# Softmax without the division: the reciprocals of the sums travel as rows through DRAM and scale the gates

## The chip, the cores and the metric

One core of a Trainium2 chip runs the kernel. The metric is the device time of the whole program in microseconds, the median of several runs. The engines are TensorE (PE; its weight loads are listed as PEld), VectorE (DVE), ScalarE (ACT), GpSimd (POOL) and SyncE (SP), which here issues all DMAs.

## The reference, cut to what matters

A layer over 1024 tokens of width 1024. Two token mixers run beside each other, each with 8 heads of 64 output columns; their outputs are gated by silu, projected, gated by a sigmoid and added.

```python
# mixer A: a chunk of 64 queries sees its own and 8 earlier chunks
s = jnp.einsum('bqhd,bkhd->bhqk', qc, kc).astype(jnp.float32) * scale + bias
p = jax.nn.softmax(s, axis=-1).astype(vc.dtype)
ya = jnp.einsum('bhqk,bkhd->bqhd', p, vc)
ya = (ya.reshape(B, S, A_WIDTH) * jax.nn.silu(a_z)) @ w_proj_a[l]
# mixer B: chunk-causal, all earlier chunks, low-rank q and kv
yb = chunk_causal_attention(q_full, k_full, kv[..., B_NOPE_DIM:])
yb = (yb.reshape(B, S, B_WIDTH) * jax.nn.silu(b_z)) @ w_proj_b[l]
mixed = jax.nn.sigmoid(g_a) * ya + jax.nn.sigmoid(g_b) * yb
```

The softmax divides each row of exponentials by its sum. The division may be done anywhere between the exponential and the projection, since it is one factor per token and head; the gate silu(z) is such a factor, too.

## The kernel before, in words

The first 110 us normalise the input and make V of mixer A and the low-rank parts of B. Then come two attention stretches, A and B, in which "dense" matmuls (the chunks of the input projection: q, k, z of each pair of heads and the output gates) are woven between the attention steps as filler for TensorE. Then the two output projections, the product with w_out and the last normalisation follow.

Heads go in pairs (four pairs per mixer; e is the head in the pair). A head has 8 steps, i = 0 to 7, each for 128 query tokens. Steps 0 to 3 are the first token half (512 tokens), steps 4 to 7 the second. In a step, `scores` makes the scores in PSUM, VectorE adds the bias (A) or masks (B) and finds the row extreme (L717, L816), and `softmax` (L825) does the rest: ScalarE takes Exp and the row sum (L828), VectorE makes 2^14 over the sum (L830, L831), ScalarE writes the high f16 half of P (L835, "hi"), VectorE the low half (L836, "lo"), and a DMA transpose issued by SyncE brings both into pT (L838). `pv` (L841) multiplies V with pT. It runs LAG_A = 3 steps (A) or LAG_B = 2 steps (B) behind the scores, from the queue of class Steps (L858). After the fourth PV of a half, `finish_y` takes y out of PSUM (L741, L742) and `finish_z` multiplies it with the gate sz on GpSimd (L748) and stores it to DRAM (L750), from where the projection's operand is loaded later. Only the last two heads of B stay on the chip (L752).

The gate sz of a pair is 128 rows (64 per head) by 512 tokens for each half. It comes from a dense chunk (`evac_silu`, L728), and its pool has two buffers. Scratch tiles of 512 columns (zt, yl, yt, weights and gates) share the ring `st` of five buffers. GpSimd also scales the bias table of each A head (L700 to L702) and splits V of B into f16 halves (L548, L551) in two stretches.

The order of the emitted steps is written out by hand (`run`, `at`, and the constants ahead of the function); the order on each engine is then settled by the framework's scheduler, which simulates the program's times.

Of the kernel before, what the change touches and what calls it, by code (L numbers as in the profile page):

```python
# [10 lines left out]
F32 = mybir.dt.float32  # L11
F32R = mybir.dt.float32r
I32 = mybir.dt.int32
AF = mybir.ActivationFunctionType
ALU = mybir.AluOpType
# [3 lines left out]
P = 128  # L19
S = 1024  # L20
# [35 lines left out]
def tile_hybrid_layer(  # L56
# [25 lines left out]
    V, A, G, SY = nc.vector, nc.scalar, nc.gpsimd, nc.sync  # L82
# [10 lines left out]
    st = ctx.enter_context(tc.tile_pool(name="st", bufs=5))  # L93
    sm = ctx.enter_context(tc.tile_pool(name="sm", bufs=6))
# [3 lines left out]
    dram = ctx.enter_context(tc.tile_pool(name="dram", bufs=1, space=DRAM))  # L98
# [3 lines left out]
    kr_d = [dram.tile([32, S], F32, name=f"kr_d{i}") for i in range(2)]  # L102
    y_d = [dram.tile([512, S], F32, name=f"y_d{i}") for i in range(2)]
    th_d = [dram.tile([D, S], F32, name=f"th_d{i}") for i in range(2)]


    ident = consts.tile([P, P], F32, name="ident")
# [102 lines left out]
    def start_ya():  # L210

        if not YA:
            tiles = {}

            def one(k, half):
                if (k // 2, 0) not in tiles:
                    for a in range(2):
                        tiles[k // 2, a] = m8.tile([P, 2, S], F32R, tag="m8", name=f"YA{k // 2}{a}")
                for a in range(2):
                    YT[0][a] = YT[0][a] or {}  # L220
                    YT[0][a][k] = tiles[k // 2, a][:, k % 2, :]
                y_part(0, k, half, YT[0][0][k], YT[0][1][k])

            YA.extend([(0, lambda k=k, half=half: one(k, half)) for k in range(4) for half in range(2)])
        return YA
# [33 lines left out]
    def proj_a(ds_):  # L259

        def one(d, half):
            ahead(0, d, half, st, AH0)
            if half == 0:
                if d < 7:
                    prep_p(0, d + 1)
                else:
                    prep_p(1, 0)
                if d % 4 == 0:
                    t = big.tile([P, 4, S], F32, tag="big", name=f"ya{d // 4}")
                    for a in range(4):  # L270
                        ya[d + a] = t[:, a, :]
            proj(0, d, half, ya[d][:, half * 512 : half * 512 + 512])

        return [(2.6, lambda d=d, half=half: one(d, half)) for d in ds_ for half in range(2)]
# [34 lines left out]
    if True:  # L309
# [203 lines left out]
        def v_units(g, v16, mixer, nm, lo_eng, ring, mx=None):  # L513
# [39 lines left out]
            def done():  # L553
                V16[2 * mixer + g] = v16

            return [(0, pre)] + [(0, lambda j=j: one(j)) for j in range(NT)] + [(0, done)]

        ln_last = {}
# [88 lines left out]
    with ExitStack() as p1:  # L647
# [88 lines left out]
        def finish_y(pair, mixer, e, half):  # L736
            h = 2 * pair.p + e
            lo = st.tile([P, 512], F32, tag="st", name=f"yl{mixer}_{h}_{half}")
            yt = st.tile([P, 512], F32, tag="st", name=f"yt{mixer}_{h}_{half}")
            r = slice(64 * e, 64 * e + 64)  # L740
            A.activation(lo[0:64, :], pair.y[64:128, :], AF.Copy, scale=us[mixer][64:128, h : h + 1])  # L741
            V.scalar_tensor_tensor(yt[r, :], pair.y[0:64, :], us[mixer][0:64, h : h + 1], lo[0:64, :], op0=ALU.mult, op1=ALU.add)  # L742
            pair.tail(e, half, yt, r)
# [78 lines left out]
            def tail(self, e, half, yt, r):  # L822
                finish_z(self, 1, e, half, yt, r)

        def softmax(pair, e, i, nm_):  # L825
            s, nm, n = pair.scores(e, i)
            su = sm.tile([P, 1], F32, tag="su", name=f"su{nm_}")
            A.activation(s[:, :n], s[:, :n], AF.Exp, scale=-1.0, bias=nm, accum_out=su)  # L828
            rc2 = sm.tile([P, 1], F32, tag="rc2", name=f"rcs{nm_}")
            V.tensor_scalar(rc2, su, 2.0 ** -14, None, op0=ALU.mult)  # L830
            V.reciprocal(rc2, rc2)  # L831
            W_ = pools["w"]
            p16 = pools["p"].tile([P, 2 * W_], F16, tag="p16", name=f"p16{nm_}")
            hi, lo = p16[:, :n], p16[:, n : 2 * n]
            A.activation(hi, s[:, :n], AF.Copy, scale=rc2)  # L835
            V.scalar_tensor_tensor(lo, s[:, :n], rc2, hi, op0=ALU.mult, op1=ALU.subtract)  # L836
            pT = pools["pt"].tile([P, 2 * W_ // P, P], F16, tag="pt", name=f"pT{nm_}")
            SY.dma_start(pT[:, : 2 * n // P, :], p16[:, : 2 * n], transpose=True)  # L838
            return pT

        def pv(pair, mixer, e, i, pT, v16):  # L841
            h = 2 * pair.p + e
            k0 = max(0, i - 4) if mixer == 0 else 0
            if i % 4 == 0:
                pair.y = ps_y.tile([P, 512], F32, tag="y", name=f"y{mixer}_{h}_{i}")
            nk = i - k0 + 1
            o = pair.y[:, (i % 4) * P : (i % 4) * P + P]
            for k in range(nk):
                for a in range(2):
                    T.matmul(o, v16[:, k0 + k, h % 4, :], pT[:, a * nk + k, :], start=(k == 0 and a == 0), stop=(k == nk - 1 and a == 1))  # L850
            if i % 4 == 3:
                finish_y(pair, mixer, e, i // 4)
# [5 lines left out]
        class Steps:  # L858
# [7 lines left out]
            def one(self):  # L866
                pair, e, i = self.seq[self.at]
                self.at += 1
                nm = f"{self.m}_{2 * pair.p + e}_{i}"
                self.q.append((pair, e, i, softmax(pair, e, i, nm)))  # L870
                if i == 6:
                    self.next_head()
                if len(self.q) > self.lag:
                    self.fin()
# [5 lines left out]

            def fin(self):
                pair, e, i, pT = self.q.pop(0)
                pv(pair, self.m, e, i, pT, V16[2 * self.m + pair.p // 2])

            def units(self, n):
# [100 lines left out]
        with ExitStack() as pb:  # L986
# [7 lines left out]
            for p in range(4):  # L994
                u = sb.units(16)
                if p < 3:
                    n = pairsB[p + 1]
# [110 lines left out]
    for j in range(NT):  # L1108
        n = 4 if j == last else 2
# [68 lines left out]
```

## Time and profile before

| | us |
|---|---|
| median of 3 runs | 876.08 (873.44 to 879.13) |
| the profiled execution | 874.21 |
| its span, first to last instruction | 872.4 |
| TensorE busy | 821.9 |
| VectorE busy | 592.2 |
| ScalarE busy | 443.0 |
| GpSimd busy | 197.6 |

All rows come from the one profiled execution. "Busy" is the time in which an engine has an instruction running; for TensorE it includes pipelined overlap. "Idle <- X" is the time that an engine stood still just before an instruction, put down to the X that ended it last.

### The profile page before, as it was taken

The page shows a single profiled execution, that of the slowest core. Times are in us where ns is not written, and L with a number is a line of the kernel's source. Part 1 is how long each engine was busy: PE and PEld are TensorE (multiplying, and loading weights), DVE is VectorE, ACT ScalarE, POOL GpSimd, SP SyncE. Part 2 cuts the span into 40 slices and gives each one's busy share as a digit, 9 for nine tenths or more (in the row PEclk, how much of TensorE's full clock was granted, in tenths as well). Part 3 has the DMA queues.
Part 4 walks back from the last instruction along what each step waited for, and adds up shares of the span by engine and source line. Part 5 has one row for each costly group of instructions (what it writes and reads, how often), then busy time and mean ns, then how long its engine had stood idle before and what let it go on. Part 6 is the DMA issues. An engine that isn't in the chain of part 4 may idle for free. (4 is left out here: it accounts for less than half of the span.)

```text
span 872.4 us, 13717 instructions
## 1 busy us (share of the span) xinstructions
PE 821.9 (94%) x4760; PEld 691.5 (79%) x4760; DVE 592.2 (68%) x1351; ACT 443.0 (51%) x857; POOL 197.6 (23%) x205
## 2 busy tenths in 40 slices
PE   5999999998998998999999999999999989999996
PEld 4999898887776876787778778787888778888886
DVE  6899856587686889845565767276637674647755
ACT  4223683476675857755563666366647552322000
POOL 6545630011111113400000521010213131331100
PEclk8999999999999999999999999999999999999999
DMA  6622023476877775674639377746886798541421
GB/s 210 209 106 77 13 62 109 142 149 141 165 138 168 139 178 96 135 202 102 152 96 200 80 166 159 162 102 140 192 199 173 186 217 289 161 151 49 160 94 48
DMA packets 185365, 124.68 MB, mean 143 GB/s; under 512 B 146161, under 2 KB 149745, under 8 KB 185297
## 3 DMA queue, kind: packets, MB, share of 16 engines
q1 hardware_dynamic: 185296, 123.82, 57.0%
q8 instruction: 37, 0.61, 0.3%
q14 instruction: 32, 0.25, 0.1%
HBM read 57.98 MB, written 22.81 MB: 93 GB/s over the span
## 5 line engine op out<-in xcount | busy, mean ns | idle before, releaser
L173 PE MATMUL dn<-hT,wh_c 128*128 128x512 f32 x512 | 204.8, 400 | 2.0 <-ACT g L294 1.3
L175 PE MATMUL dn<-hT,wl_c 128*128 128x512 f32 x512 | 201.5, 394 | 0.0
L174 PE MATMUL dn<-hT,wh_c 128*128 128x512 f32 x512 | 201.4, 393 | 0.0
L748 POOL TENSOR_TENSOR yt<-yt,sz 64x512 f32<-64x512 f32 x32 | 43.6, 1362 | 328.0 <-DVE yt L742 263.8
L173 PEld LDWEIGHTS dn<-hT,wh_c 128*128 128x128 f32 x512 | 97.0, 190 | 20.2 <-ACT g L294 1.8
L175 PEld LDWEIGHTS dn<-hT,wl_c 128*128 128x128 f32 x512 | 96.7, 189 | 20.0
L174 PEld LDWEIGHTS dn<-hT,wh_c 128*128 128x128 f32 x512 | 97.0, 189 | 17.6
L132 DVE TENSOR_TENSOR wl_c<-wr_c,wh_c 128x512 fp32r<-128x512 f32 x64 | 47.8, 746 | 77.4 <-ACT wh_c L131 71.2
L131 ACT ACTIVATE wh_c<-wr_c 128x512 fp32r<-128x512 f32 x64 | 40.2, 629 | 82.4 <-DMA wr_c<-in_wch_dram 63.2
L836 DVE SCALAR_TENSOR_TENSOR p<-sbs,rcs,p 128x128 f16<-128x128 f32 (+3 forms) x64 | 57.1, 901 | 24.2 <-ACT p L835 22.3
L828 ACT ACTIVATE sbs<-sbs,nmb 128x128 f32<-128x128 f32 (+3 forms) x64 | 49.5, 774 | 33.4 <-DVE sbs L816 30.1
L836 DVE SCALAR_TENSOR_TENSOR p<-ss,rcs,p 128x640 f16<-128x640 f32 (+2 forms) x64 | 50.7, 803 | 9.2 <-ACT p L835 8.1
L828 ACT ACTIVATE ss<-ss,nm 128x640 f32<-128x640 f32 (+2 forms) x64 | 44.3, 692 | 23.1 <-DVE nm L717 20.6
L835 ACT ACTIVATE p<-sbs,rcs 128x128 f16<-128x128 f32 (+3 forms) x64 | 48.5, 769 | 12.8 <-ACT sbs L828 6.8
L850 PE MATMUL y<-pT,v16b 128*128 128x128 f16 x576 | 43.7, 222 | 9.8 <-DMA pT<-p 9.8
L175 PE MATMUL ops<-wo,mixT 128*128 128x512 f32 (+1 forms) x144 | 52.9, 367 | 0.0
L850 PEld LDWEIGHTS <-v16b 128*128 128x128 f16 x576 | 33.9, 99 | 23.8 <-issue 22.2
L174 PE MATMUL ops<-wo,mixT 128*128 128x512 f32 (+1 forms) x144 | 52.7, 366 | 0.0
L173 PE MATMUL ops<-wo,mixT 128*128 128x512 f32 (+1 forms) x144 | 51.5, 368 | 0.0
L816 DVE TENSOR_SCALAR_CACHE_REDUCE sbs<-sb 128x128 f32<-128x128 f32 (+3 forms) x64 | 47.9, 754 | 1.3
L717 DVE CUSTOM_DVE_ANT_0 ss<-sa,tb 128x640 f32<-128x640 f32 (+2 forms) x64 | 41.3, 652 | 8.9 <-PE sa L713 5.2
L850 PE MATMUL y<-pT,v16a 128*128 128x128 f16 x480 | 37.4, 220 | 9.6 <-DMA pT<-p 9.6
(248 smaller groups left out, 1847.8 us busy)
## 6 DMA issues: line engine op xcount, KB each, us to landing
wr_c<-in_wch_dram SPq DMA_DIRECT2D x64, 256.0 KB, 3.2
th_d<-g SPq DMA_DIRECT2D x32, 256.0 KB, 2.9
th<-th_d SPq DMA_DIRECT2D x32, 256.0 KB, 3.7
h_d<-xt SPq DMA_DIRECT2D x8, 512.0 KB, 2.6
sX<-sQ SPq DMA_DIRECT2D x16, 256.0 KB, 4.2
sXb<-bQ SPq DMA_DIRECT2D x16, 256.0 KB, 4.3
r<-h_d SPq DMA_DIRECT2D x8, 512.0 KB, 3.6
wor<-in_wo_dram SPq DMA_DIRECT2D x16, 256.0 KB, 3.0
```

Of the source, the lines that this page charges most:

```text
L131: A.activation(hi, raw, AF.Copy)
L132: (eng or V).tensor_tensor(lo, raw, f(hi), op=ALU.subtract)
L173: T.matmul(ps, ah, bh, start=start, stop=False)
L174: T.matmul(ps, ah, bl, start=False, stop=False)
L175: return T.matmul(ps, al, bh, start=False, stop=stop).ins
L717: V.tensor_tensor_reduce(s[:, :n].rearrange("p (b w) -> p b w", b=nb), ps[:, :nb, :w], self.tb[e][:, 640 - n : 640].rearrange("p (b w) -> ...
L748: G.tensor_tensor(yt[r, :], yt[r, :], pair.sz[half][r, :], op=ALU.mult)
L816: V.tensor_scalar(s[:, :n].rearrange("p (b w) -> p b w", b=nb), ps[:, :nb, :w], -B_SCALE, None, op0=ALU.mult, op1=ALU.min, accum_out=nm,)
L828: A.activation(s[:, :n], s[:, :n], AF.Exp, scale=-1.0, bias=nm, accum_out=su)
L835: A.activation(hi, s[:, :n], AF.Copy, scale=rc2)
L836: V.scalar_tensor_tensor(lo, s[:, :n], rc2, hi, op0=ALU.mult, op1=ALU.subtract)
L850: T.matmul(o, v16[:, k0 + k, h % 4, :], pT[:, a * nk + k, :], start=(k == 0 and a == 0), stop=(k == nk - 1 and a == 1))
```

## The change

P is no longer divided by its row sums. hi and lo are the exponentials times the constant 2^14. The sums of four steps gather in the four columns of one tile. After the fourth step VectorE takes their reciprocals in one instruction, and GpSimd issues a DMA that writes them as a row of 512 tokens to a DRAM tile (`sums_out`). Two steps later (at i = 5 for the first half, at i = 1 of the next head for the second) `norm` issues, again from GpSimd, a read of that row broadcast to 64 partitions, and GpSimd multiplies the gate sz by it in place. `finish_z` is as before, so y is divided there by way of the gate. The last half of a mixer is normed in `fin`, just ahead of its PV product.

```diff
+    rc_d = [dram.tile([8, S], F32, name=f"rc_d{i}") for i in range(2)]
...
-        def softmax(pair, e, i, nm_):
+        def softmax(mixer, pair, e, i, nm_):
             s, nm, n = pair.scores(e, i)
-            su = sm.tile([P, 1], F32, tag="su", name=f"su{nm_}")
-            A.activation(s[:, :n], s[:, :n], AF.Exp, scale=-1.0, bias=nm, accum_out=su)
-            rc2 = sm.tile([P, 1], F32, tag="rc2", name=f"rcs{nm_}")
-            V.tensor_scalar(rc2, su, 2.0 ** -14, None, op0=ALU.mult)
-            V.reciprocal(rc2, rc2)
+            if i % 4 == 0:
+                sums[pair, e] = sm.tile([P, 4], F32, tag="su", name=f"su{nm_}")
+            su = sums[pair, e]
+            A.activation(s[:, :n], s[:, :n], AF.Exp, scale=-1.0, bias=nm, accum_out=su[:, i % 4 : i % 4 + 1])
...
-            A.activation(hi, s[:, :n], AF.Copy, scale=rc2)
-            V.scalar_tensor_tensor(lo, s[:, :n], rc2, hi, op0=ALU.mult, op1=ALU.subtract)
+            A.activation(hi, s[:, :n], AF.Copy, scale=2.0 ** 14)
+            V.scalar_tensor_tensor(lo, s[:, :n], 2.0 ** 14, hi, op0=ALU.mult, op1=ALU.subtract)
...
+            if i % 4 == 3:
+                sums_out(mixer, pair, e, i // 4, su)
...
+        def sums_row(mixer, pair, e, half):
+            return rc_d[mixer][2 * pair.p + e : 2 * pair.p + e + 1, half * 512 : half * 512 + 512]
...
+        def sums_out(mixer, pair, e, half, su):
...
+            rc = sm.tile([P, 4], F32, tag="rc", name=f"rc{nm}")
+            V.reciprocal(rc, su)
+            G.dma_start(sums_row(mixer, pair, e, half).rearrange("o (a b) -> (o b) a", a=4), rc)
+            open_.add((pair, e, half))
...
+        def norm(mixer, pair, e, half):
...
+            r = slice(64 * e, 64 * e + 64)
+            rb = st.tile([P, 512], F32, tag="st", name=f"rb{nm}")
+            G.dma_start(rb[r, :], sums_row(mixer, pair, e, half).broadcast_to([64, 512]))
+            G.tensor_tensor(pair.sz[half][r, :], pair.sz[half][r, :], rb[r, :], op=ALU.mult)
...
-                self.q.append((pair, e, i, softmax(pair, e, i, nm)))
+                self.q.append((pair, e, i, softmax(self.m, pair, e, i, nm)))
+                if i in (1, 5) and self.at > 2:
+                    past = self.seq[self.at - 3]
+                    norm(self.m, past[0], past[1], past[2] // 4)
...
             def fin(self):
                 pair, e, i, pT = self.q.pop(0)
+                if i % 4 == 3 and (pair, e, i // 4) in open_:
+                    norm(self.m, pair, e, i // 4)
```

## Rows read from the trace of the kernel before

**Rows 1.** The page's head and its first part: span, and busy time by engine.
```profile
span 872.4 us, 13717 instructions
PE 821.9 (94%) x4760; PEld 691.5 (79%) x4760; DVE 592.2 (68%) x1351; ACT 443.0 (51%) x857; POOL 197.6 (23%) x205
```
**Rows 2.** Table of stretches: length, busy time by engine, granted clock, DMA share, GB/s.
```profile
168.00:396.00 228.00, 213.91 (x1338) 175.90 (x1337) 172.32 (x418) 154.70 (x304) 43.50 (x55) 0.99 0.70 148
396.00:722.00 326.00, 309.92 (x1800) 254.29 (x1800) 201.53 (x503) 187.40 (x342) 53.89 (x46) 0.99 0.68 156
```
**Rows 3.** TensorE's waits: total us, how many, the longest.
```profile
PE y L850 <- DMA pT<-p: 19.4, 23, 2.4
...
PE sa L712 <- DVE nm L717: 3.7, 2, 2.3
PE sb L809 <- DVE sbs L816: 3.5, 4, 2.0
...
PE sb L809 <- DVE rcs L830: 1.3, 1, 1.3
```
**Rows 4.** Timeline of one softmax step of mixer A: start, length, engine, instruction.
```profile
238.09 0.19 ACT L828 ACTIVATION_READ_ACCUMULATOR ss<-ss,nm 128x1 f32 x1
...
238.31 0.15 DVE L830 TENSOR_SCALAR rcs<-su 128x1 f32<-128x1 f32 x1
...
238.50 0.16 DVE L831 RECIPROCAL rcs<-rcs 128x1 f32<-128x1 f32 x1
...
238.74 0.83 ACT L835 ACTIVATE p<-ss,rcs 128x640 f16<-128x640 f32 x1 [0.47 <-ACT ss L828]
```
**Rows 5.** Groups by line and shape: busy us, mean ns of one, idle before.
```profile
L831 DVE RECIPROCAL rcs<-rcs 128x1 f32<-128x1 f32 x128 | 20.7, 163 | 3.4
...
L830 DVE TENSOR_SCALAR rcs<-su 128x1 f32<-128x1 f32 x128 | 19.2, 151 | 26.6 <-ACT sbs L828 17.7 <-ACT ss L828 7.0
...
L550 ACT ACTIVATE v16b<-vs_b 128x256 f16<-128x256 f32 x16 | 6.2, 405 | 0.1
...
L835 ACT ACTIVATE p<-sbs,rcs 128x256 f16<-128x256 f32 x8 | 4.0, 501 | 2.7 <-issue 1.6 <-ACT sbs L828 1.1
```
**Rows 6.** Timeline of TensorE: first and last of the 23 waits for pT.
```profile
177.39 0.38 PE L850 MATMUL y<-pT,v16a 128*128 128x128 f16 x4 [0.79 <-DMA pT<-p]
...
713.46 0.72 PE L850 MATMUL y<-pT,v16b 128*128 128x128 f16 x10 [1.90 <-DMA pT<-p]
```
**Rows 7.** Groups by line: two of GpSimd's products.
```profile
L748 POOL TENSOR_TENSOR yt<-yt,sz 64x512 f32<-64x512 f32 x32 | 43.6, 1362 | 328.0 <-DVE yt L742 263.8 <-DVE rcs L830 18.5 <-DVE sb L813 17.9
...
L548 POOL TENSOR_TENSOR vs_b<-v16b,vsc_b 128x256 f32<-128x256 f32 x16 | 15.2, 958 | 31.5 <-ACT vsc_b L539 28.5 <-DVE sz L733 2.4 <-DVE wl_kn L132 0.2
```
**Rows 8.** Timeline at the end of a mixer A half: an issue on SyncE, the sum.
```profile
240.43 0.42 SPq L699 DMA_DIRECT2D tb<-in_relb_dram  x1
...
241.05 0.19 ACT L828 ACTIVATION_READ_ACCUMULATOR ss<-ss,nm 128x1 f32 x1
```
**Rows 9.** DMA: packets, queue with its share of 16 engines, issues with landing times.
```profile
DMA packets 185365, 124.68 MB, mean 143 GB/s; under 512 B 146161, under 2 KB 149745, under 8 KB 185297
...
q1 hardware_dynamic: 185296, 123.82, 57.0%
...
y_d<-yt SPq DMA_DIRECT2D x28, 128.0 KB, 2.5
...
pT<-p SPq DMA_TRANSPOSE x128, 3.4
```
**Rows 10.** The view of the tile pT, its landing line.
```profile
DMA to landing us min/median/max: 2.3/3.4/6.8
```
**Rows 11.** Timeline: the gate product of that half, and B's last sum and gate product.
```profile
253.90 1.81 POOL L748 TENSOR_TENSOR yt<-yt,sz 64x512 f32<-64x512 f32 x1 [8.39 <-DVE yt L742]
...
711.96 0.19 ACT L828 ACTIVATION_READ_ACCUMULATOR sbs<-sbs,nmb 128x1 f32 x1
...
724.91 1.29 POOL L748 TENSOR_TENSOR yt<-yt,sz 64x512 f32<-64x512 f32 x1 [11.93 <-DVE yt L742]
```

More of the change, by code (lines that the diff above doesn't have):

```diff
@@ L834, in softmax @@
             hi, lo = p16[:, :n], p16[:, n : 2 * n]
-            A.activation(hi, s[:, :n], AF.Copy, scale=rc2)
-            V.scalar_tensor_tensor(lo, s[:, :n], rc2, hi, op0=ALU.mult, op1=ALU.subtract)
+            A.activation(hi, s[:, :n], AF.Copy, scale=2.0 ** 14)
+            V.scalar_tensor_tensor(lo, s[:, :n], 2.0 ** 14, hi, op0=ALU.mult, op1=ALU.subtract)
             pT = pools["pt"].tile([P, 2 * W_ // P, P], F16, tag="pt", name=f"pT{nm_}")
             SY.dma_start(pT[:, : 2 * n // P, :], p16[:, : 2 * n], transpose=True)
-            return pT
+            if i % 4 == 3:
+                sums_out(mixer, pair, e, i // 4, su)
+            return pT
+        sums, open_ = {}, set()
+        def sums_row(mixer, pair, e, half):
+            return rc_d[mixer][2 * pair.p + e : 2 * pair.p + e + 1, half * 512 : half * 512 + 512]
+        def sums_out(mixer, pair, e, half, su):
+            nm = f"{mixer}_{2 * pair.p + e}_{half}"
+            rc = sm.tile([P, 4], F32, tag="rc", name=f"rc{nm}")
[3 more added lines that the diff above has]
+        def norm(mixer, pair, e, half):
+            nm = f"{mixer}_{2 * pair.p + e}_{half}"
+            open_.remove((pair, e, half))
+            r = slice(64 * e, 64 * e + 64)
+            rb = st.tile([P, 512], F32, tag="st", name=f"rb{nm}")
+            G.dma_start(rb[r, :], sums_row(mixer, pair, e, half).broadcast_to([64, 512]))
+            G.tensor_tensor(pair.sz[half][r, :], pair.sz[half][r, :], rb[r, :], op=ALU.mult)
         def pv(pair, mixer, e, i, pT, v16):
```

## The prediction

> **What bounds the kernel now.** I read the page's first part, then the table of stretches, then TensorE's waits, then one softmax step in the timeline. TensorE is busy for 821.9 of 872.4 us [rows 1], so at most 50 us can be had from it, and only where it waits. The change works in the two attention stretches alone, from 168 to 396 us (mixer A) and from 396 to 722 us (mixer B). There TensorE is busy for 213.9 of 228 and 309.9 of 326 us [rows 2]: 30.2 us idle. VectorE (172 and 202 us), ScalarE (155 and 187 us) and GpSimd (43 and 54 us) have room on the average. What matters is therefore the latency of a step, not the sum of its work. The table of TensorE's waits says which latency: 19.4 us in 23 waits of the PV product for its transposed P (pT), then 8.5 us in 7 waits of the scores matmul for VectorE (3.7 + 3.5 + 1.3) [rows 3]. So the last link ahead of TensorE is the chain Exp, reciprocal, hi, lo, transpose.
>
> **What the change removes.** In each of the 128 steps, ScalarE's hi copy waits for two tiny VectorE instructions on the sum. The timeline of a step shows it: the accumulator read ends at 238.28, the scaling runs at 238.31, the reciprocal at 238.50, and hi starts only at 238.74, with an idle of 0.47 us put down ahead of it [rows 4]. After the change hi depends on Exp alone, which ran before it on the same engine: 0.46 us of latency is gone. hi's scale also becomes a constant. Two ScalarE copies of 128x256 to f16 differ in just that: 405 ns without a scale from memory, 501 ns with one [rows 5]. I take 0.09 us; zero is the lower end. lo's scalar becomes a constant too, which I take at nothing. A step's pT is then ready 0.55 us earlier. VectorE loses 128 x (151 + 163 ns) = 40.2 us [rows 5] and gets 32 reciprocals of four columns back, 32 x 0.163 = 5.2 us.
>
> **What that is worth on TensorE.** I went through the 23 waits for pT one by one (the first is 0.79 us, the last 1.90 us [rows 6]) and took from each the smaller of its length and 0.55 us: 13 are longer and give 7.2 us, the 10 shorter ones sum to 3.0 us. That is 10.2 us. The waits for VectorE shrink by at most the 0.31 us that each step sheds there: 7 x 0.31 = 2.2 us. Together 12.4 us. The ends are 27.9 us (all these waits gone) and 0: the order of instructions on each engine is laid out by a planner that simulates the kernel, and a planner that sees pT earlier may put the PV product earlier, so that it waits as long as before.
>
> **What it adds on GpSimd.** Per token half and head (32 in all) there are two DMA issues, two waits on landings, and one 64x512 product. The product is the same shape as the gate product that runs now, 1362 ns [rows 7], so 43.6 us in all. A DMA issued by GpSimd does not occur before the change. The nearest row is an issue on the SyncE queue, 0.42 us [rows 8]. [...] I take 0.42 us, since that row is the same kind of instruction: 64 x 0.42 = 27 us. GpSimd then works 97 + 44 + 27 = 168 of 554 us, plus waits. From the sum to the scaled gate the chain is 0.16 (reciprocal) + 0.42 + 2.5 (landing of the store of y to DRAM) + 0.42 + 3.4 (landing of pT, for the broadcast read) + 1.36 = 8.3 us [rows 5, 7 to 9]. The cover is the time from the end of the accumulator read of a half's last step to the gate product that needs the result: 241.24 to 253.90 = 12.7 us in A, and 712.15 to 724.91 = 12.8 us at the very end of B [rows 8, 11]. So 4.4 us are left and I cost the chain at nothing. With both landings at 6.8 us it is 16.0 us and the gate product comes 3 us late. That product feeds a store whose reader comes much later, and at the end of B TensorE has projections to run. What is queued behind a waiting GpSimd is the bias table of the next head and the splitting of V, on which a ScalarE copy waits. By the code that is 16 products of L548 (0.96 us [rows 7]), one per step, in 16 of the 128 steps: 32 x 16/128 = 4 halves fall there. At 5.9 us of landings each, that is at most 24 us on ScalarE. TensorE would see a part of it, because PV runs two or three steps behind the scores. I take 0 and keep 10 us for the range. The broadcast tile also holds one of the five buffers of `st`, for 0.42 + 3.4 + 1.36 = 5.2 us: 32 x 5.2 = 166 of 5 x 554 buffer-us, 6%. At nothing, too; without that cover ScalarE's evacuation of a dense chunk would wait for a buffer and hold one of the two dense PSUM tiles. The gate must be there one step earlier than now. Its dense chunk is the first of a pair, and its first half is four of some 24 units, so it lies well ahead of step 5.
>
> **What it adds on the DMA engines.** They are busy for 0.70 and 0.68 of the two stretches [rows 2], so this is the fullest resource after TensorE. A row of sums goes out as 512 elements of 4 bytes, each a packet of its own, 32 on each of 16 engines. A mean packet now takes 0.57 x 872.4 us x 16 / 185296 = 43 ns [rows 9], so a scatter takes 1.38 us of every engine. The broadcast read of 128 KB runs at 156/0.68 = 229 GB/s [rows 2], 0.57 us. That is 1.95 us per half, 62 us in all, and the share goes to about 0.80. It falls on the resource that delivers pT. TensorE waits for 23 of 128 pT, 18%. If every scatter and read holds one pT up for its whole length, 32 x 1.95 x 0.18 = 11.2 us come back; if the packets slip between, none. I take the middle, 5.6 us. SyncE's own queue gains no instruction, and its pT issues, which wait for lo, come earlier.
>
> **The sum.** 874.2 us (the profiled execution; span 872.4 and 1.8 around it) - 12.4 + 5.6 = 867.4 us. The profiled execution is 1.9 us under the median of 876.08, so against the median the forecast is 869 us, 0.8% faster.
>
> **Rivals.**
> *The gain is replanned away.* TensorE is 94% busy, and a planner may spend a shorter chain on an earlier PV product. For it: the waits now are short (19.4 us in 23) although each step's chain has some microseconds, so the order already sits close to the data. Against it: the waits come from landings later than planned, and the change shortens the part that the landing follows. Time: 876, or up to 880 with some of the packet cost.
> *The whole of it comes through.* Less waiting, VectorE 35 us lighter and no packet cost: 876 - 12.4 = 864; with half of the other waits, (27.9 - 12.4)/2 = 8 us, gone as well, 856.
> *The scatter is dear, and the kernel ends slower.* The mechanism is one: packets of 4 bytes hold the DMA engines while pT is in flight. With the same half weight it decides where 32 x 0.18 x 0.5 x (32 p + 0.57 us) = 12.4 us, at p = 117 ns a packet, 2.7 times today's mean. At 250 ns it is 8.57 us per half and 24.7 us back: 876 + 12 = 888 us. At 150 ns the engines' free 31% (172 us, 5.4 us per half) would be used up as well. For it: no packet of 4 bytes written to DRAM is in this trace. Against it: the mean of 43 ns is made mostly of small ones, 146161 of 185365 being under 512 B [rows 9]. [...]
> [...]
> *That it does not do what it says* would be a hi copy that still waits for VectorE; the diff leaves it no such operand, so I give this no chance of its own.
>
> **How the numbers follow.** Forecast (862 to 873) 0.45; replanned away (873 to 881) 0.20; everything comes through (852 to 862) 0.14; dear packets or a GpSimd that holds ScalarE (881 to 900) 0.21. A change of 1% (8.8 us) is about what a measurement of this kernel can tell from none. Under 867.3 us lie the whole third case and somewhat under half of the first, 0.14 + 0.21 = 0.35. Over 884.8 us lies most of the last, 0.17. Between them is 0.48. The range leaves out the outer parts of the two end cases: 857 to 888.
>
> **What the profile after would show.** Right: the idle ahead of the hi copy for VectorE gone, the two tiny lines replaced by 32 reciprocals, PV's waits for pT near 9 to 15 us, scores waits under 7 us, GpSimd near 240 us busy with the gate's scaling ending before the gate product starts, DMA share near 0.80. Replanned: the same shorter steps, but PV's waits as long as now. Dear packets: a second DMA queue with some 16000 packets and a large share of the engines, and the median landing of pT well over 3.4 us. The prediction is wrong where GpSimd's issue of 512 elements takes many microseconds, so that the chain passes 12.7 us, or where ScalarE shows new waits for GpSimd in the V stretches.

## The result: 1051.5 us, 19.8% slower

The changed kernel takes 1051.53 us (median of 4 runs, 1043.12 to 1057.87) against 877.61 us (4 runs, 873.44 to 880.02): a ratio of 1.1975, 95% interval 1.1916 to 1.2035. The forecast was 869 us with 888 us as its upper end.

The profiled execution after the change has a span of 1041.3 us. The head of its page, and its DMA queues (packets, MB, share of 16 engines), answer to [rows 1, 9]:

```profile
span 1041.3 us, 13686 instructions
...
PE 878.4 (84%) x4760; PEld 733.3 (70%) x4760; DVE 567.5 (54%) x1127; ACT 434.3 (42%) x857; POOL 287.1 (28%) x301
...
DMA packets 187924, 128.94 MB, mean 124 GB/s; under 512 B 147696, under 2 KB 151280, under 8 KB 187856
...
q1 hardware_dynamic: 185296, 123.82, 61.3%
q0 software_dynamic: 2560, 4.26, 2.2%
```

TensorE idles 162.9 us in place of 50.5, and the same 4760 matmuls are busy for 56.5 us longer. The old queue q1 moves the same 185296 packets and the same 123.82 MB as before, but each holds its engine for 0.613 x 1041.3 x 16 / 185296 = 55 ns on the average, 43 ns before [rows 9]. The new queue q0 takes only 2.2%. So the new transfers take little of the engines by themselves, and the old ones take longer; that the first causes the second is shown under spread below.

The stretches of mixers A and B, now 308 and 408 us long (228 and 326 before [rows 2]; the columns are the length, the busy us of TensorE, its weight loads, VectorE, ScalarE and GpSimd, the granted clock, the DMA share and GB/s):

```profile
168.00:476.00 308.00, 241.34 (x1329) 197.47 (x1328) 161.51 (x305) 149.71 (x302) 87.15 (x103) 0.87 0.78 116
476.00:884.00 408.00, 333.78 (x1812) 270.26 (x1811) 189.48 (x392) 183.79 (x344) 99.26 (x93) 0.92 0.75 130
```

Of the 168.9 us by which the span grew, 162 lie here. The DMA share rises to 0.78 and 0.75 while the GB/s fall from 148 and 156 to 116 and 130: the engines are taken up for longer and move less. The granted clock falls from 0.99 of full speed [rows 2] to 0.87 and 0.92 in the same stretches, where TensorE stands still most.

The waits (engine, line, what it waited for: us, how often, the longest), to be read beside [rows 3]:

```profile
PE y L874 <- DMA pT<-p: 112.5, 40, 6.9
...
ACT wh_c L132 <- DMA wr_c<-in_wch_dram: 109.5, 27, 11.3
ACT p L835 <- DMA pT<-p: 77.3, 22, 9.8
...
POOL rb L862 <- DMA rc_d<-rc: 127.8, 14, 12.0
POOL sz L863 <- DMA rb<-rc_d: 102.3, 28, 11.5
```

TensorE waits for pT for 112.5 us, 19.4 before. ScalarE's hi copy waits for pT as well: it writes into a P buffer that an older transpose still reads, so a late transpose stops the softmax steps behind it, too. ScalarE's longest wait is for the dense weights (wr_c), and it has grown as well; before it was

```profile
ACT wh_c L131 <- DMA wr_c<-in_wch_dram: 63.2, 31, 3.9
```

The list of DMA issues (KB each, median us to landing; pT took 3.4 [rows 10]):

```profile
rb<-rc_d POOLq DMA_DIRECT2D x32, 128.0 KB, 4.0
...
pT<-p SPq DMA_TRANSPOSE x128, 5.8
...
rc_d<-rc POOLq DMA_DIRECT2D x32, 2.0 KB, 9.4
```

A store of 2 KB lands after 9.4 us, a read of 128 KB after 4.0 us. The timeline around one store (start, length, engine, instruction, idle before it) puts the two together:

```profile
250.19 5.20 SPq L838 DMA_TRANSPOSE pT<-p  x3
...
250.38 0.81 POOL L853 DMA_DIRECT2D rc_d<-rc  x1 [0.80 <-DVE rc L852]
...
252.10 0.39 PE L174 MATMUL dn<-hT,wh_c 128*128 128x512 f32 x1
...
252.17 0.20 ACT L831 ACTIVATION_READ_ACCUMULATOR ss<-ss,nm 128x1 f32 x1
...
252.40 0.74 ACT L835 ACTIVATE p<-ss 128x640 f16<-128x640 f32 x1
...
260.12 0.80 PE L874 MATMUL y<-pT,v16a 128*128 128x128 f16 x6 [4.99 <-DMA pT<-p]
...
260.16 0.74 ACT L835 ACTIVATE p<-ss 128x640 f16<-128x640 f32 x1 [5.69 <-DMA pT<-p]
260.39 0.54 POOL L862 DMA_DIRECT2D rb<-rc_d  x1 [9.20 <-DMA rc_d<-rc]
...
261.62 0.63 PE L174 MATMUL dn<-hT,wh_c 128*128 128x512 f32 x1
```

The store is issued at 250.38. Then TensorE (idle 4.99 us), ScalarE (5.69 us) and GpSimd (9.20 us) start again within 0.27 us of one another: the store lands at 259.86, the first transpose issued beside it (at 250.19) at 260.07, and the two behind that one (at 252.43 and 254.06) at 262.77 and 262.94. The two ScalarE rows at 252 also show the intended edit at work: the accumulator read ends at 252.37 and hi starts at 252.40, where 0.46 us lay between them in the step shown before [rows 4].

The stop costs TensorE a second time. Before it the granted clock is 1.00; after the 4.99 us of standing still it is 0.50 from 260 to 264, and matmuls of one shape (L174) take 0.63 us in place of 0.39. In 266 to 268 us it is 1.00 again. TensorE stands still for 4 us or more 14 times between 168 and 884 us, and in the second microsecond after each of these stops the clock is 0.50. The same table for short stretches around this one (a packet counts where it starts, so a DMA share can pass 1):

```profile
250.00:255.00 5.00, 5.00 (x27) 4.14 (x26) 4.27 (x9) 4.44 (x9) 0.81 (x1) 1.00 0.65 118
260.00:262.00 2.00, 1.88 (x10) 1.83 (x10) 0.97 (x2) 0.74 (x1) 0.54 (x1) 0.50 1.34 129
262.00:264.00 2.00, 2.00 (x6) 1.57 (x5) 0.69 (x2) 0.92 (x2) 0.00 (x0) 0.50 0.86 169
...
266.00:268.00 2.00, 2.00 (x19) 1.76 (x18) 1.30 (x3) 1.98 (x4) 0.54 (x1) 1.00 0.40 131
```

### The profile page after: what moved, and what is told of

Same layout as the page of the kernel before. It is cut to its first block, busy times and chain, and to the rows that moved or that the text cites. A ratio compares the mean times of both kernels' runs of the same rounds, so it can differ in the third digit from the quotient of the medians.

```text
span 1041.3 us, 13686 instructions
## 1 busy us (share of the span) xinstructions
PE 878.4 (84%) x4760; PEld 733.3 (70%) x4760; DVE 567.5 (54%) x1127; ACT 434.3 (42%) x857; POOL 287.1 (28%) x301
## 3 DMA queue, kind: packets, MB, share of 16 engines
q1 hardware_dynamic: 185296, 123.82, 61.3%
q0 software_dynamic: 2560, 4.26, 2.2%
## 4 chain that ended last, share of the span: by engine, by line
PE 32%; DMA 27%; DVE 4%; issue 3%; ACT 2%; SPq 2%; POOL 1%; DVEq 0%; ACTq 0%; POOLq 0%
DMA pT<-p 18%; DMA wr_c<-in_wch_dram 8%; PE y L874 3%; PE ops L174 3%; PE ops L176 3%; PE ops L175 3%; PE dn L174 3%; PE dn L175 3%; PE pj L174 3%; PE dn L176 3%; PE pj L175 3%; PE pj L176 3%; DVE p L836 1%; DVE wl_c L133 1%; PE sb L812 1%
## 5 line engine op out<-in xcount | busy, mean ns | idle before, releaser
L174 PE MATMUL dn<-hT,wh_c 128*128 128x512 f32 x512 | 214.4, 419 | 6.1 <-DVE sK L664 2.4
L175 PE MATMUL dn<-hT,wh_c 128*128 128x512 f32 x512 | 209.3, 409 | 0.0
L174 PEld LDWEIGHTS dn<-hT,wh_c 128*128 128x128 f32 x512 | 102.0, 199 | 26.9 <-ACT g L295 2.7
L175 PEld LDWEIGHTS dn<-hT,wh_c 128*128 128x128 f32 x512 | 101.6, 199 | 18.3
L874 PE MATMUL y<-pT,v16a 128*128 128x128 f16 x480 | 45.1, 244 | 61.0 <-DMA pT<-p 60.9
L132 ACT ACTIVATE wh_c<-wr_c 128x512 fp32r<-128x512 f32 x64 | 40.2, 628 | 134.8 <-DMA wr_c<-in_wch_dram 109.5
L874 PEld LDWEIGHTS <-v16a 128*128 128x128 f16 x480 | 33.9, 110 | 71.3 <-issue 68.7
L836 DVE SCALAR_TENSOR_TENSOR p<-sbs,p 128x128 f16<-128x128 f32 (+3 forms) x64 | 52.7, 824 | 55.8 <-ACT p L835 53.7
L836 DVE SCALAR_TENSOR_TENSOR p<-ss,p 128x640 f16<-128x640 f32 (+2 forms) x64 | 55.2, 870 | 43.1 <-ACT p L835 42.5
L862 POOL DMA_DIRECT2D rb<-rc_d x32 | 17.4, 543 | 215.8 <-DMA rc_d<-rc 127.8
L863 POOL TENSOR_TENSOR sz<-sz,rb 64x512 f32<-64x512 f32 x32 | 44.7, 1398 | 106.5 <-DMA rb<-rc_d 102.3
L831 ACT ACTIVATE sbs<-sbs,nmb 128x128 f32<-128x128 f32 (+3 forms) x64 | 49.4, 772 | 50.7 <-DVE sbs L817 50.5
L835 ACT ACTIVATE p<-sbs 128x128 f16<-128x128 f32 (+3 forms) x64 | 43.6, 681 | 45.6 <-DMA pT<-p 44.6
L176 PE MATMUL ops<-wo,mixT 128*128 128x512 f32 (+1 forms) x144 | 52.9, 367 | 0.0
```

The source lines that it names most:

```text
L132: A.activation(hi, raw, AF.Copy)
L174: T.matmul(ps, ah, bh, start=start, stop=False)
L175: T.matmul(ps, ah, bl, start=False, stop=False)
L176: return T.matmul(ps, al, bh, start=False, stop=stop).ins
L835: A.activation(hi, s[:, :n], AF.Copy, scale=2.0 ** 14)
L836: V.scalar_tensor_tensor(lo, s[:, :n], 2.0 ** 14, hi, op0=ALU.mult, op1=ALU.subtract)
```

## The experiments

Two theories stood first. *Dear scatter* (T in the expectations): the stores of 4-byte pieces hold up pT, whatever else changes. *Another part or another order* (G, P, O): any DMA from GpSimd, GpSimd's waits, the reads, the scaling, or a different plan by the scheduler. All kernels are edits of the changed one. The lines that differ are shown, shortened at "...", or told in words where an earlier diff shows the like. A time without a ratio is one run.

**no_norm: only the shorter chain.** No reciprocals, stores, reads or scaling.

```diff
-            V.reciprocal(rc, su)
-            G.dma_start(sums_row(...)..., rc)
...
-            G.dma_start(rb[r, :], sums_row(...).broadcast_to([64, 512]))
-            G.tensor_tensor(pair.sz[half][r, :], pair.sz[half][r, :], rb[r, :], op=ALU.mult)
```

> The changed kernel without reciprocals, stores, reads and the scaling of the gates (y stays undivided, so this leaves out the division). Theory T (the stores in 4-byte pieces hold the DMA engines while pT is in flight): only the gain of the shorter step is left, about 864 us (856 to 876), pT lands in 3.4 us as before and PV waits 9 to 15 us for it. Rival G (any DMA issued by GpSimd holds pT up): the same here. Rival O (the planner's new order of instructions is what costs): still above 1000 us, with PV waiting about 100 us.

873.27 us, ratio 0.9933 (0.9896 to 0.9971). This is all that the shorter chain is worth: 0.67%, some 6 us, in the upper part of T's range. TensorE's wait for pT is no shorter than before:

```profile
PE y L868 <- DMA pT<-p: 21.5, 17, 2.7
```

**scatter_only and sp_scatter: the store alone, and its queue.** The first drops the read and the scaling from the changed kernel. The second keeps everything and issues the store from SyncE.

```diff
-            G.dma_start(sums_row(mixer, pair, e, half).rearrange("o (a b) -> (o b) a", a=4), rc)
+            SY.dma_start(sums_row(mixer, pair, e, half).rearrange("o (a b) -> (o b) a", a=4), rc)
```

> The changed kernel with the reciprocals and the 4-byte stores, but without the broadcast read and the scaling of the gates (leaves out the division). T: nearly the whole loss stays, 1020 to 1050 us, pT lands in 5 to 6 us in the median. G: half the GpSimd DMAs are left, so about half the loss, near 960 us. A rival P (GpSimd's waits for landings and the late gates cost): no wait is left on GpSimd, so about 870 us.

> The changed kernel with the 4-byte stores issued by SyncE instead of GpSimd; same bytes, same pieces. T: as slow as the change or slower, 1030 us and more, because the pieces are the same and their issue now stands in the queue of the transposes. G: only the reads are left on GpSimd, near 960 us.

The stores alone give 1027.55 us, 154 us over no_norm, which the whole change exceeds by 178 us. From SyncE it is 1067.4 us, and the store lands no sooner, so GpSimd's queue isn't the cause:

```profile
rc_d<-rc SPq DMA_DIRECT2D x32, 2.0 KB, 9.7
```

Waits for pT and queues of scatter_only:

```profile
PE y L871 <- DMA pT<-p: 115.4, 32, 8.5
```
```profile
q1 hardware_dynamic: 185296, 123.82, 64.1%
q0 software_dynamic: 1024, 0.07, 0.5%
...
rc_d<-rc POOLq DMA_DIRECT2D x32, 2.0 KB, 9.5
```

The stores' own records take 0.5% of 1025.7 us, 5.1 us of each engine for all 32. Against no_norm TensorE idles 113.6 us more (162.1 against 48.5) and is busy 39.9 us longer (863.6 against 823.7) at a mean granted clock of 0.936 against 0.983. Of the 153.5 us between the two spans, three quarters are standing still and one quarter is slower matmuls.

**rows16: larger pieces.** The token order in DRAM is changed, so that the four sums of a partition lie together: 128 pieces of 16 bytes. The product reads the row with a stride.

```diff
-            G.dma_start(sums_row(mixer, pair, e, half).rearrange("o (a b) -> (o b) a", a=4), rc)
+            G.dma_start(sums_row(mixer, pair, e, half).rearrange("o (b a) -> (o b) a", a=4), rc)
...
-            G.tensor_tensor(pair.sz[half][r, :], pair.sz[half][r, :], rb[r, :], op=ALU.mult)
+            z4 = pair.sz[half][r, :].rearrange("p (a b) -> p a b", a=4)
+            G.tensor_tensor(z4, z4, rb[r, :].rearrange("p (b a) -> p a b", a=4), op=ALU.mult)
```

> The changed kernel with the sums stored as 128 pieces of 16 bytes (the four columns of a token row side by side), still from GpSimd; the read is as before and the scaling reads the broadcast tile with a stride of four. T with a price per piece: a quarter of the loss of 175 us and the gain of 12, about 905 us (885 to 940). T with a price per byte or per DMA: no better than 1040 us. G and P: about 1050 us.

900.42 us, ratio 1.0231 (1.0163 to 1.03): the whole of the change with 151 us less. The store lands after 2.7 us. The time falls into the range that a price per piece gave (885 to 940), but by luck: rows16_store below shows that these stores cost nothing.

**spread: small pieces, far apart.** As scatter_only, but the 512 pieces of 4 bytes lie 64 bytes apart.

```diff
-    rc_d = [dram.tile([8, S], F32, name=f"rc_d{i}") for i in range(2)]
+    rc_d = [dram.tile([8, 16 * S], F32, name=f"rc_d{i}") for i in range(2)]
...
-            G.dma_start(sums_row(...).rearrange("o (a b) -> (o b) a", a=4), rc)
+            G.dma_start(sums_row(...).rearrange("o (a b c) -> (o b) a c", a=4, c=16)[:, :, 0:1],
+                        rc.rearrange("p (a c) -> p a c", c=1))
```

> As scatter_only (1027.55 us; stores, no read, no scaling, so the division is left out), but each 4-byte piece goes to a place of its own, 64 bytes from the next, so 512 pieces of 4 bytes stand in 32 KB instead of side by side in 2 KB. T-piece (each small piece has its price): as slow, 1010 to 1040 us, landing near 9 us. T-line (pieces from different engines that fall into the same few bytes of DRAM wait for one another): near no_norm's 873 us, 870 to 900, landing near 3 us.

871.71 us. The same number of pieces of the same size from the same partitions costs nothing that can be seen beside no_norm's 873.27. TensorE's waits for pT and the queues of spread:

```profile
PE y L871 <- DMA pT<-p: 18.7, 19, 3.2
...
q1 hardware_dynamic: 185296, 123.82, 56.9%
q0 software_dynamic: 1024, 0.07, 0.6%
...
rc_d<-rc POOLq DMA_DIRECT2D x32, 2.0 KB, 3.1
```

q0 takes as much as in scatter_only; q1 takes 56.9% of 869.9 us in place of 64.1% of 1025.7. All engines and SyncE have exactly the same order of instructions in the two kernels; only DRAM addresses differ. That excludes the planner's order for these 156 us, and leaves a third theory: pieces that fall into the same stretch of DRAM wait for one another. I took 64 bytes for that stretch.

How the stores reach TensorE can be counted in the two traces. In scatter_only 59 of the 128 transposes are issued while a store is pending; they land after 8.7 us in the median, the other 69 after 3.4 us. So do dense weights (wr_c): 19 after 6.8 us, 45 after 3.0 us. In spread 34 transposes are issued beside a store, and they land after 3.7 us, the other 94 after 3.5 us. The same count in the changed kernel gives 62 transposes after 8.3 us and 66 after 3.5 us, and dense weights 17 after 8.2 us and 47 after 3.3 us.

**one_col and own4: what makes the crowd.** one_col stores one column, 128 pieces side by side in 512 bytes. own4 stores all four, in rows16's order but with gaps in the source, so that they remain 512 pieces; each 64 bytes then come from 4 partitions in place of 16.

```diff
-            G.dma_start(sums_row(...).rearrange("o (a b) -> (o b) a", a=4), rc)
+            G.dma_start(sums_row(...).rearrange("o (a b) -> (o b) a", a=4)[:, 0:1], rc[:, 0:1])
```
```diff
-            rc = sm.tile([P, 4], F32, tag="rc", name=f"rc{nm}")
+            rc = sm.tile([P, 4, 2], F32, tag="rc", name=f"rc{nm}")
...
-            G.dma_start(sums_row(...).rearrange("o (a b) -> (o b) a", a=4), rc)
+            G.dma_start(sums_row(...).rearrange("o (b a) -> (o b) a", a=4), rc[:, :, 0])
```

> As scatter_only, but one column of the sums is stored instead of four: 128 pieces of 4 bytes side by side (leaves out three quarters of the sums and the division). T-piece: a quarter of the loss of 154 us, 900 to 920 us, landing 2 to 4 us as with the 128 pieces of 16 bytes. A price per store whatever its pieces: 1000 us and more.

> Stores only, as scatter_only (1027.55 us; the division is left out), again 512 pieces of 4 bytes in 2 KB, but placed so that the 16 pieces of each 64 bytes come from four neighbouring partitions (the four columns of each side by side, read with a gap in SBUF so that each piece stays 4 bytes) and not from 16 partitions. T-crowd (many small pieces into the same few bytes wait for one another whoever sends them): still 1000 us and more, landing 8 to 9 us. T-engines (only pieces of different DMA engines in the same few bytes do): 870 to 885 us, landing near 3 us.

one_col takes 1004.11 us with a landing of 8.5 us: a quarter of the pieces, nearly the whole price, where a price per piece gave 900 to 920 us. own4 takes 1022.3 us and lands after 8.9 us. Neither the number of pieces nor the number of partitions behind each 64 bytes is the price; it is the crowd in DRAM.

**rows16_store.** scatter_only with rows16's store.

> Stores only, in 128 pieces of 16 bytes (the division is left out). If the parts add up, rows16 (900) less what read_only loses against no_norm (about 15 us): 880 to 887 us. If the 16-byte store is free and the rest of rows16's loss comes from the longer wait ahead of the read: 870 to 876 us.

871.74 us, landing 2.7 us: the stores in 16-byte pieces are free, and the 27 us by which rows16 lies over no_norm come from its reads and its scaling.

**pitch8 and pitch16.** As spread, with c = 2 and c = 4 in place of 16: pieces 8 and 16 bytes apart.

> As the kernel that stores sums and reads nothing, but the 512 pieces of 4 bytes lie 8 bytes apart in 4 KB of DRAM, so 8 of them share 64 bytes (16 in the changed kernel: 1027.6 us and a median landing of 9.5 us; one: 871.7 us and 3.1 us). Theory that each piece waits for the others of its 64 bytes, at one price a piece: the store lands after about 2.7 + (8 - 4) x (9.5 - 2.7)/(16 - 4) = 5.0 us, pT's median lies between 3.5 and 4.5 us, the time between 885 and 960 us. Rival that only pieces that touch one another are dear (each write then spans into the next piece's bytes): no piece touches another here, so it lands near 3.1 us and the time is 870 to 876 us. Rival that the window is the whole 512 bytes and more: between, nearer to 9 us.

> The same with the pieces 16 bytes apart in 8 KB, four to 64 bytes. Theory of the shared 64 bytes: as with 16-byte pieces, four to 64 bytes, which landed after 2.7 us: landing 2.7 to 3.5 us, pT's median 3.4 to 3.7 us, 868 to 880 us. [...]

910.03 us with a landing of 5.2 us, and 882.81 us with 3.7 us, a little over what the shared 64 bytes gave (868 to 880 us, 3.5 us). The price grows with the crowd and needs no touching pieces. At 16 bytes it is small: no_norm's ten runs reach 881.15 us, and pT's waits are 18.4 us.

**few64 and few128: in which unit?** As scatter_only, with 16 of the partitions: 64 pieces (four columns), and 16 pieces (one column). 16 pieces still share 64 bytes, but only 16 share 512.

```diff
-            G.dma_start(sums_row(...).rearrange("o (a b) -> (o b) a", a=4), rc)
+            G.dma_start(sums_row(...).rearrange("o (a b) -> (o b) a", a=4)[0:16, :], rc[0:16, :])
```

> As the kernel that stores all 512 sums and reads nothing, but only 16 of the 128 partitions are stored: 64 pieces of 4 bytes, in four stretches of 64 bytes, 512 bytes apart. The rest of the row stays unwritten. Within 64 bytes the crowd is as before (16 pieces side by side), within 512 bytes there are 16 pieces in place of 128. Theory that the pieces of the same 64 bytes wait for one another, some 0.5 us each: landing 7 to 9.5 us, pT's median over 4.5 us, 950 to 1030 us. Rival that the unit is 512 bytes (128 pieces in one took 8.5 us, 66 ns a piece): 16 pieces add 1.1 us, landing 2.5 to 4 us, pT's median 3.4 to 3.7 us, 868 to 885 us.

> The same with one column: 16 pieces of 4 bytes in one stretch of 64 bytes, and nothing else is stored. Theory of the shared 64 bytes: landing 7 to 9.5 us and over 930 us even so, because one crowd is as slow as four. Rival of 512 bytes: landing 2 to 4 us, 868 to 885 us. A landing of 7 us or more beside a time near 872 us would say that the wait is there but that a single crowd doesn't hold up the others' transfers.

872.56 and 872.84 us, both with a landing of 2.6 us (the lines are few64's):

```profile
pT<-p SPq DMA_TRANSPOSE x128, 3.6
...
rc_d<-rc POOLq DMA_DIRECT2D x32, 0.2 KB, 2.6
```

So my theory that pieces of the same 64 bytes wait for one another, 0.5 us each, falls: sixteen of them cost nothing. The rival with a unit of 512 bytes had the numbers right. These stores are also smaller than the others and come from 16 partitions, so a price that needs many partitions in one stretch isn't excluded. The stores side by side, without reads:

| kernel | pieces x bytes | apart, bytes | in 512 bytes | store lands, us | pT lands, us | time, us |
|---|---|---|---|---|---|---|
| few128 | 16 x 4 | 4 | 16 | 2.6 | 3.5 | 872.84 |
| few64 | 64 x 4 | 4 | 16 | 2.6 | 3.6 | 872.56 |
| spread | 512 x 4 | 64 | 8 | 3.1 | 3.5 | 871.71 |
| rows16_store | 128 x 16 | 16 | 32 | 2.7 | 3.4 | 871.74 |
| pitch16 | 512 x 4 | 16 | 32 | 3.7 | 3.5 | 882.81 |
| pitch8 | 512 x 4 | 8 | 64 | 5.2 | 3.9 | 910.03 |
| one_col | 128 x 4 | 4 | 128 | 8.5 | 5.1 | 1004.11 |
| own4 | 512 x 4 | 4 | 128 | 8.9 | 5.3 | 1022.3 |
| scatter_only | 512 x 4 | 4 | 128 | 9.5 | 5.3 | 1027.55 |

(Landings are medians; one run each. TensorE, VectorE and SyncE have the same order of instructions in all nine; ScalarE too, but for a few lines in the first two.)

**read_only, reads_nomult, mult_only, mult_dve: the rest.** Without stores: read_only reads a row written once at the start and scales; reads_nomult reads and doesn't scale; mult_only scales by a tile that is in SBUF anyway and has no DMA of its own; mult_dve does that product on VectorE.

```diff
-            G.tensor_tensor(pair.sz[half][r, :], pair.sz[half][r, :], rb[r, :], op=ALU.mult)
+            G.tensor_tensor(pair.sz[half][r, :], pair.sz[half][r, :], f(hT[0][0][r, 0, 0:512]), op=ALU.mult)
```

> The changed kernel without the stores; the row is written once at the start (with a constant, so the division is left out), and the broadcast reads, GpSimd's waits for them and the scaling of the gates stay. T: little more than no_norm, 873 to 880 us. P (GpSimd's reads, waits and late gates are what rows16 loses against no_norm, 27 us): 890 to 900 us.

> As read_only (888.6 us), but the gates are not scaled: reads of a constant row alone (the division is left out). If the reads' traffic is what read_only loses: 883 to 890 us. If GpSimd's products and waits are: 870 to 877 us.

> No store and no read; the gates are scaled on GpSimd by a tile that lies in SBUF (a wrong factor, so the division is left out). If GpSimd's 32 products and what they hold back are what read_only loses: 883 to 890 us. If the reads are: 870 to 877 us.

> The kernel without stores and reads, whose 32 products (64x512, with a factor that is in SBUF already) run on VectorE in place of GpSimd. With them on GpSimd it took 884.3 us, without them 873.3 us, and the lo half in mixer A went from 733 to 832 ns. Theory that GpSimd's reads of SBUF slow VectorE's lo half and so pT: lo is near 733 ns again and the time falls to 872 to 878 us, although VectorE has 32 products more (some 0.6 us each). Rival that it is the product as such, a task more that the scheduler has to place and a gate that is ready later: 880 to 890 us, lo near 733 ns all the same.

read_only 888.6 us, between its two ranges. reads_nomult 888.71 us, ratio 1.0131 (1.009 to 1.0172). mult_only 884.34 us, 1.0093 (1.0058 to 1.0127). mult_dve 882.1 us, 1.0052 (1.0032 to 1.0072). Against no_norm's 0.9933 a product costs 1.6% on GpSimd (14 us) and 1.2% on VectorE (10 us), the reads 2.0% (17 us), and both together 2.1% in read_only (888.6 beside 876.1, 18 us) and 3.0% in rows16 (26 us). They don't add up. (The products of mult_dve take 833 ns each, where I had put 0.6 us.) The lo half of mixer A in no_norm, mult_only and mult_dve (us in all, mean ns):

```profile
L836 DVE SCALAR_TENSOR_TENSOR p<-ss,p 128x640 f16<-128x640 f32 (+2 forms) x64 | 46.7, 733 | 18.2 <-ACT p L835 17.6
```
```profile
L836 DVE SCALAR_TENSOR_TENSOR p<-ss,p 128x640 f16<-128x640 f32 (+2 forms) x64 | 52.8, 832 | 15.7 <-ACT p L835 15.0
```
```profile
L836 DVE SCALAR_TENSOR_TENSOR p<-ss,p 128x640 f16<-128x640 f32 (+2 forms) x64 | 46.0, 722 | 18.3 <-ACT p L835 17.0 <-DMA pT<-p 0.2
```

GpSimd's products do slow VectorE's lo (733 to 832 ns), and it recovers with the product on VectorE (722 ns). But the time recovers by only some 4 us, and the two intervals overlap: that theory explains the smaller part at most. The rest comes with the product as such, and with the read as such. The scheduler's orders differ between these kernels, and nothing here separates the task from the order; that stays open.

**pe_rows: no small pieces at all.** TensorE turns the 128x4 reciprocals into 4 rows, ScalarE copies them, and SyncE stores four pieces of 512 bytes.

```diff
-            G.dma_start(sums_row(...).rearrange("o (a b) -> (o b) a", a=4), rc)
+            ps = ps_dn.tile([P, 512], F32, tag="dn", name=f"rp{nm}")
+            T.transpose(ps[0:4, 0:P], rc, ident)
+            rr = sm.tile([4, P], F32, tag="rr4", name=f"rr{nm}", bufs=2)
+            A.activation(rr, ps[0:4, 0:P], AF.Copy)
+            SY.dma_start(sums_row(...).rearrange("o (a b) -> (o a) b", a=4), rr)
```

> The whole computation with the sums turned into rows on TensorE: one transpose of 128x4 per half (32 in all, about 0.1 us each), a ScalarE copy of 4x128, and a store by SyncE of 4 pieces of 512 bytes; read and scaling as in the change. T: stores no longer cost, so no_norm's 873 plus 3 us on TensorE plus the read's share, 876 to 888 us, pT landing 3.4 to 3.6 us. P: as rows16, 895 to 905 us.

908.65 us, ratio 1.039 (1.0336 to 1.0445), above both ranges. pT's waits are 31.9 us, near rows16's 31.0. Each turn takes TensorE 0.27 us, not 0.1 us, and holds a dense PSUM tile; no run separates these from the rest. It is no better than rows16; no version of the whole change beats the kernel before.

## Why the prediction was wrong, step by step

**The step that failed** is the cost of the scatter: "a scatter takes 1.38 us of every engine", from 32 packets at the mean of 43 ns, and with half weight 5.6 us in all. The store measured 154 us (no_norm to scatter_only). Its own packets take less than I gave them, 5.1 us / 32 = 0.16 us of an engine each. There are fewer of them, too: 1024 for 32 stores, 2 an engine on the average in place of 32, and few128's 16 pieces make as many. (Issued from SyncE, sp_scatter, the stores add 16896 packets to q1.) The price is in the other queue: while a crowded store is pending, the transposes and weights stall with it (scatter_only: 8.7 us in place of 3.4 and 6.8 us in place of 3.0). I let a store hold one pT for its packets' time; in scatter_only the stores hold 59, for some 5 us each. A cost per packet, at any p, misses this, because one_col has a quarter of the pieces at nearly the same price, and spread has all of them at none.

**The weight was wrong, too.** I let a delay count where TensorE had waited before, in 18% of the steps. But a delay of 5 us is more than the order leaves room for (before, pT has been there for 2.2 us on the average when its PV starts): TensorE's waits for it go from 23 to 40 and the longest from 2.4 to 6.9 us, and ScalarE joins them (77.3 us) because its P buffers aren't read out. And after the long stops TensorE's clock was lower (0.50 after the 14 of 4 us or more in the changed kernel; 0.936 in scatter_only's mean, 0.983 in no_norm's), to which I gave no term: 39.9 us of scatter_only's loss are slower matmuls.

**The rival "the scatter is dear"** had place and direction right, and of its signs the landing of pT (well over 3.4 us: 5.8). The other sign, some 16000 packets with a large share of the engines, did not come: q0 has 2560 with 2.2%. And its price was "at 250 ns it is 8.57 us per half and 24.7 us back". The landing of 9.4 us is near that 8.57 us by chance, since the 8.57 us were packets' time on every engine; what it did to TensorE was six times the 24.7 us. The argument against it, that the mean of 43 ns is made mostly of small packets, speaks of the packets' own time, and that is not where the price lies.

Pieces of 4 bytes that lie apart cost nothing here (spread: 3.1 us, 871.71 us), so the size alone doesn't set the price. 128 pieces in 512 bytes take 8.5 us (one_col) and 16 pieces 2.6 us (few128). What makes the crowded ones wait is not shown.

**The gain** was sized at 12.4 us and is 0.67%, some 6 us. hi's scale was worth what I took, 0.09 us. The same copy before and in no_norm (us in all, mean ns):

```profile
L835 ACT ACTIVATE p<-ss,rcs 128x640 f16<-128x640 f32 x32 | 25.6, 820 | 1.6 <-ACT ss L828 0.9 <-DVE rcs L831 0.2
```
```profile
L835 ACT ACTIVATE p<-ss 128x640 f16<-128x640 f32 x32 | 23.4, 732 | 0.6
```

VectorE's busy time falls from 592.2 to 553.0 us in no_norm, 39.2 us less (40.2 forecast for the two removed instructions). The chain got shorter by more than I forecast: the one step that I read, with 0.46 us ahead of hi, is the shortest of the 128. On the average of all steps the time from the sum's end to pT's landing falls from 7.5 to 6.2 us, by 1.3 us and not 0.55. But the waits for pT stay at 21.5 us. The term "I took from each the smaller of its length and 0.55 us" failed, and the rival "replanned away" was right, in its mechanism too: in no_norm the first PV matmul of a step starts 8.5 us after the sum, 9.7 us before, with 46 in place of 52 TensorE instructions between them, so that pT has been there for 2.3 us on the average as against 2.2.

**GpSimd.** The products measured 44.7 us (43.6 forecast). The issues, put at 0.42 us after a row of SyncE, are 0.81 us for the store and 0.54 us for the read, 43 us in all in place of 27. By lines of the changed kernel (busy us, mean ns):

```profile
L863 POOL TENSOR_TENSOR sz<-sz,rb 64x512 f32<-64x512 f32 x32 | 44.7, 1398 | 106.5 <-DMA rb<-rc_d 102.3 <-PE sa L714 4.0
...
L853 POOL DMA_DIRECT2D rc_d<-rc x32 | 26.0, 812 | 87.5 <-DVE rc L852 76.7 <-DMA qr<-qr_d 4.5 <-DVE vrcol_b L535 4.0
...
L862 POOL DMA_DIRECT2D rb<-rc_d x32 | 17.4, 543 | 215.8 <-DMA rc_d<-rc 127.8 <-issue 65.8 <-DMA th_d<-g 16.5
```

The chain of 8.3 us "at nothing" passes its cover of 12.7 us because of the store, whose 9.4 us exceed even the 6.8 us of pT's slowest landing before [rows 10]; with rows16's store, which lands after 2.7 us, the same stretch at the end of B takes 11.2 us. In the changed kernel:

```profile
871.33 0.81 POOL L853 DMA_DIRECT2D rc_d<-rc  x1
884.13 0.53 POOL L862 DMA_DIRECT2D rb<-rc_d  x1 [11.99 <-DMA rc_d<-rc]
888.90 1.28 POOL L863 TENSOR_TENSOR sz<-sz,rb 64x512 f32<-64x512 f32 x1 [4.24 <-DMA rb<-rc_d]
890.25 1.29 POOL L749 TENSOR_TENSOR yt<-yt,sz 64x512 f32<-64x512 f32 x1
```

18.9 us from the store's issue to the product's end, and the gate product follows at once. Costing products and reads at nothing was wrong as well: 14 and 17 us by themselves. The cover that I named hides their latency; it doesn't hide what they do to VectorE's lo (733 to 832 ns) and to the DMA share in mixer A (0.70 to 0.75 in 168 to 396 us of reads_nomult; in 396 to 722 us it is 0.66, as in no_norm). mult_dve, which has the same products on VectorE and lo at 722 ns, puts what the slower lo is worth at some 4 us, if it is worth anything.

**The account.** 877.6 - 6 (chain) + 154 (stores) + 24 (reads and scaling, scatter_only to the changed kernel) = 1049.6 us, measured 1051.5. The last two terms are differences between neighbouring kernels, so the sum has to come near; it does not test them.

## What to carry to other kernels

Before a column of sums is written to DRAM as a row, count the pieces that fall into the same 512 bytes: 32 stores of 4-byte pieces side by side cost 154 us here, 16 bytes per piece or 64 bytes of distance made the same store free. Price a new DMA by what it does to the transfers in flight beside it, and when a row of the trace shows nothing like it, let the range follow the slowest thing it could stall. A shorter chain ahead of a busy engine may leave its waits as they were: here the scheduler placed the PV products earlier by as much as the chain got shorter.

## What the hardware showed that I had not expected

The landing of a store of 512 pieces of 4 bytes goes from 3.1 to 9.5 us by its layout in DRAM alone, with the packets' own engine time about the same (0.6% of 869.9 us and 0.5% of 1025.7 us). The other queue's packets take 57 ns in place of 43 ns on the average meanwhile. Within 512 bytes, 8 to 16 pieces of 4 bytes cost nothing that can be seen (landing after 3.1 and 2.6 us; 871.71 to 872.84 us in all), 32 add about half a microsecond (3.7 us), 64 about 2 us (5.2 us) and 128 about 6 us (8.5 to 9.5 us). That the unit is exactly 512 bytes isn't shown: few64 and few128 also send fewer pieces than the others, from fewer partitions, and 16-byte pieces, 32 to 512 bytes, are as quick as 2.7 us.
